# The rows of the residual scaled by their norm on ScalarE in place of VectorE

## The chip, the cores and the metric

One core of a Trainium2 chip runs the whole program. The metric is the device time of one execution in microseconds (us). The time before is the median of three runs.

## The reference

One layer of a backbone for 128 context tokens and 2048 latent tokens, 17 tiles of 128 rows, with 1024 features. What matters here is the second half of the block, and within it the norm:

```python
def rmsnorm(x, w):
    xf = x.astype(jnp.float32)
    y = xf * lax.rsqrt(jnp.mean(xf * xf, axis=-1, keepdims=True) + EPS)
    return (y * w).astype(x.dtype)

x = x + ga1 * o                                        # o: the mixer's output projection
h = rmsnorm(x, norm_ffn_l) * (1.0 + sc2) + sh2
x = x + ga2 * (jnp.square(jax.nn.relu(h @ w_ff1_l)) @ w_ff2_l)
```

The mixer ahead of it runs a gated delta rule over chunks in both directions (the scans) beside a chunked gating MLP. After the block comes one more norm.

## The kernel before

**Stages.** The program first projects all tokens, then scans the sequence forwards and backwards, and last runs the MLP. The backward scan goes through the tiles from 16 down. With each tile it finishes the mixer's output (gate, transposes, output projection, residual add), and for the tiles 16 to 9 it also makes the operands of the MLP. For the tiles 8 to 0 the operands are made in the MLP stage, between the products for the tiles above.

**The MLP's operands.** `h2_steps` makes them for one tile, in steps: the squares of the residual rows and their sum (L836, ScalarE), the sum and rsqrt (L844 and L177 on VectorE, L178 on POOL, which leaves `r`, one number for a row), the scaling of two half rows of 512 by `r` (`scale2`, L849), four transposes on TensorE for each half (L856), and a scale and bias for each feature on the way out of PSUM (L859). The transposed tiles are then combined in pairs (L880), split into a high and a low part (`opH` by a cast on ScalarE, L874; `opL` by a subtraction on VectorE, L875) and stored to DRAM (L877), from where the MLP loads them as `hop`.

**Splits.** Matrix products run three times, high by high, high by low and low by high (L220, L221, L222). So every operand has a cast on ScalarE and a subtraction on VectorE.

**What surrounds the scaling in the scan stage.** On VectorE: `L1437` and `L1438` multiply the output projection by its gate and add it to the residual rows `x`; `L1395` finishes the factors `rr` for the norm of the scan's output, and `L1400` scales that output, `o`, by them (four heads, four instructions); `L1056` and `L1178` belong to the scan (its values, and the masks of the triangular inverse); `L1028` prepares the next chunk. On TensorE: `L1415` transposes `o` and `ob` (the output of the gating MLP); `L1189`, `L1195` and `L1175` are steps of the inverse, `L1062` and `L994` of the scan; `L1246` ends an inverse that `L1239` on VectorE feeds. On ScalarE: `L1419` takes the transposed `o` and `ob` out of PSUM as the high part of the next product (VectorE's `L1420` makes the low part), `L1198` casts the inverse's `Y` and `X` for TensorE, `L1065` copies the scan's `vn`, and `L1021`, `L1022` and `L1067` prepare decay factors.

**What sets the order.** The steps are written in the order of a table of times for each scan step, with some orders between engines set by hand; then a scheduler orders the instructions of all engines by a model of their times. So a step that changes its engine can move other instructions. Each engine runs its instructions in that order, and waits in place for what an instruction needs. All loads and stores are issued on SP's queue.

Of the kernel before, what the change touches and what calls it, by code (L numbers as in the profile page):

```python
# [13 lines left out]
AF = mybir.ActivationFunctionType  # L14
# [48 lines left out]
def hybrid_step(  # L63
# [7 lines left out]
    V, A, G, T = nc.vector, nc.scalar, nc.gpsimd, nc.tensor  # L71
# [9 lines left out]
    def cond(t):  # L81
        return 0 if t == 0 else 1

    def f32(ap):
        return ap.bitcast(F32)
# [88 lines left out]
    def rsqrt_cols(out, ss, n, scale, eps):  # L174
        t = smp.tile([P, 72], F32, tag="rsq", name="rsq", bufs=2)
        np_ = ss.shape[0]
        V.tensor_scalar(out=t[:np_, :n], in0=ss, scalar1=scale, scalar2=eps, op0=ALU.mult, op1=ALU.add)  # L177
        G.tensor_tensor(out=out, in0=t[:np_, :n], in1=nhalf[:np_, :n], op=ALU.pow)  # L178
# [102 lines left out]
    with ExitStack() as ph:  # L281
# [108 lines left out]
        for t in BLOCKS[0]:  # L390
            x = p1.tile([P, D], F32, tag="x", name="x", bufs=3)
# [368 lines left out]
        for bi in range(len(BLOCKS)):  # L760
# [8 lines left out]
            for n, (gi, h) in enumerate(order):  # L769
                u = us[n] if bi == 0 and n < 3 else feature_tile(blk, bi, gi, h)  # L770
# [48 lines left out]
    def h2_steps(t, psum, tmp, wide=w512, part=None, half=None, src=None, own=None):  # L819


        u = {}
        cd = cond(t)
        wide, part, half = wide, part or wide, half or w512

        def rows():
            u["x"] = [wide("x"), wide("x")]
            for n in range(2):
                load(out=u["x"][n], in_=x2_d[t * P : (t + 1) * P, n * 512 : (n + 1) * 512])

        def squares():
            if src:
                u["x"] = src()
            u["ss"] = smp.tile([P, 2], F32, tag="ss2", name="ss2")
            for n in range(2):
                A.activation(tmp(), u["x"][n], AF.Square, accum_out=u["ss"][:, n : n + 1])  # L836
            if t % 2:
                u["y"] = [part("y"), part("y")]
                for h, y in enumerate(u["y"]):
                    load(out=y.rearrange("p (k d) -> p k d", k=4), in_=h2_d[t + 1][:, h * 4 : h * 4 + 4, :])  # L840

        def norm2():
            u["r"] = smp.tile([P, 1], F32, tag="r", name="r")
            V.tensor_tensor(out=u["ss"][:, 0:1], in0=u["ss"][:, 0:1], in1=u["ss"][:, 1:2], op=ALU.add)  # L844
            rsqrt_cols(u["r"], u["ss"][:, 0:1], 1, 1.0 / D, EPS)

        def scale2():
            for n in range(2):
                V.tensor_scalar_mul(u["x"][n], u["x"][n], u["r"])  # L849

        def trans2(half):
            def f():
                ps = psum()
                ev = wide("ev")
                for i in range(4):
                    T.transpose(ps[:, i * P : (i + 1) * P], u["x"][half][:, i * P : (i + 1) * P], ident)  # L856
                for i in range(4):
                    k = half * 4 + i
                    A.activation(ev[:, i * P : (i + 1) * P], ps[:, i * P : (i + 1) * P], AF.Identity,  # L859
                                 scale=a2[:, cd, k : k + 1], bias=b2[:, cd, k : k + 1])  # L860
                if own:
                    own(ev, half)
                elif t in h2_d:
                    store(out=h2_d[t][:, half * 4 : half * 4 + 4, :], in_=ev.rearrange("p (k d) -> p k d", k=4))
                else:
                    u[half] = ev
            return f

        def put(o, src):

            c = (t - 1) % 8 // 2 * P
            dst = hop_d[t <= 8, o][:, :, :, c : c + P]
            h, lo = half("opH", F32R), half("opL", F32R)
            A.copy(h, src)  # L874
            V.tensor_tensor(out=lo, in0=src, in1=f32(h), op=ALU.subtract)  # L875
            for i, piece in enumerate((h, lo)):
                store(out=dst[:, :, i, :], in_=f32(piece).rearrange("p (k d) -> p k d", k=4))  # L877

        def sub(a, b, out=None):
            V.tensor_tensor(out=a if out is None else out, in0=a, in1=b, op=ALU.subtract)  # L880

        def plain():
            put(1, u[0])
            put(2, u[1])
            u["d"] = part("d")
            sub(u["y"][1], u["y"][0], u["d"])

        def third():
            put(3, u["y"][1])
            put(7, u["d"])  # L890
            sub(u["y"][0], u[0])

        def fifth():
            put(5, u["y"][0])
            sub(u["y"][1], u["y"][0])

        def sixth():
            put(6, u["y"][1])
            sub(u[1], u["y"][1])

        def fourth():
            put(4, u[1])

        ops = [plain, third, fifth, sixth, fourth] if t % 2 else []
        return ([] if src else [rows]) + [squares, norm2, scale2, trans2(0), trans2(1)] + ops

    def sraw():
# [19 lines left out]
    with ExitStack() as ph:  # L927
# [551 lines left out]
        for i, u in enumerate(units):  # L1479
# [9 lines left out]
            if c == 0:  # L1489
# [3 lines left out]
                n = len(steps)  # L1493
# [118 lines left out]
    class Unit:  # L1612
# [6 lines left out]
        def load(self, i, kh):  # L1619
            for q in range(2):  # L1620
                self.raw[i, kh, q] = r = w512("raw")
                r0, c0 = kh * 512 + q * 256, self.jp * 512 + i * 256
                load(out=r.rearrange("p (a c) -> p a c", a=2),
                     in_=w_ff1[0, r0 : r0 + 256, c0 : c0 + 256].rearrange("(a p) c -> p a c", p=P))
# [354 lines left out]
    for p, (o, n, m) in enumerate(seq):  # L1979
        u = units[n]  # L1980
# [126 lines left out]
```

## Time and profile before

| | |
|---|---|
| median of 3 runs | 2574.07 us (2570.79 to 2575.09) |
| the profiled execution | 2574.06 us |
| its span, from the first to the last instruction | 2572.3 us |
| TensorE (PE) busy | 2536.5 us |
| VectorE (DVE) busy | 1782.1 us |
| ScalarE (ACT) busy | 1192.8 us |
| GpSimd (POOL) busy | 315.1 us |
| granted TensorE clock | 0.999 |

In the rows below, a name such as L849 is a line of the kernel, and `out<-in` are tiles. A row of the timeline starts with the time in the span and the length in us; a bracket at its end is the time for which its engine had been idle, and what released it. A row of the waits gives who waited for whom, the sum in us, the number of times, and the longest. A row of a group of instructions gives the busy time in us and the mean of one in ns, then the idle time ahead of them and its releasers. An engine's idle time matters only where another engine waits for it in the end.

### The profile page before, as it was taken

To read this page: it belongs to the slowest core of one execution; us is meant where nothing else is said; L and a number is where in the kernel's file an instruction comes from. 1 tells how busy PE (TensorE), PEld (TensorE's weight loads), DVE (VectorE), ACT (ScalarE), POOL (GpSimd) and SP (SyncE) were. 2 spreads that over 40 slices of the span, in tenths; PEclk is the share of its full clock that TensorE was granted. 3 is DMA by queue.
4 is the path that set the end of the run, shared out by engine and by line. 5 is a ranking of instruction groups with operands and counts; after the bars stand their busy time and mean duration, and the time that the engine had idled before them with its cause. 6 is when DMAs were issued, how large, how long until landed. Compare 5 with 4: busy or idle time off the path is not lost.

```text
span 2572.3 us, 43717 instructions
## 1 busy us (share of the span) xinstructions
PE 2536.5 (99%) x15296; PEld 2132.5 (83%) x15296; DVE 1782.1 (69%) x3525; ACT 1192.8 (46%) x2758; POOL 315.1 (12%) x512
## 2 busy tenths in 40 slices
PE   8999999999999999999999999999999999999998
PEld 4999999788888788778888888888888888888887
DVE  5777746667667788885587886677674445684874
ACT  4755545554545566763355553333243333243441
POOL 3112112222222233331000000000000000000000
PEclk9999999999999999999999999999999999999999
DMA  8966637755556758896778788445599778686773
GB/s 285 299 225 205 191 126 219 246 161 171 171 169 179 228 185 270 279 304 209 274 219 249 221 289 279 140 147 152 180 299 323 267 258 296 241 259 211 232 253 105
DMA packets 533859, 579.77 MB, mean 225 GB/s; under 512 B 35500, under 2 KB 366684, under 8 KB 530054
## 3 DMA queue, kind: packets, MB, share of 16 engines
q1 hardware_dynamic: 533638, 576.98, 69.3%
q8 instruction: 120, 1.97, 0.3%
q14 instruction: 101, 0.83, 0.1%
HBM read 397.62 MB, written 179.22 MB: 224 GB/s over the span
## 4 chain that ended last, share of the span: by engine, by line
PE 55%; DVE 1%; issue 1%; DMA 0%; ACT 0%; POOL 0%; DVEq 0%; POOLq 0%; ACTq 0%
PE f L220 17%; PE f L221 17%; PE f L222 17%; PE pj L220 1%; PE pj L222 1%; PE pj L221 1%; PE f L856 0%; PE pd L994 0%; PE pd L1098 0%; PE pd L1099 0%; DMA hop_d<-opL 0%; PE pm L1415 0%; PE pd L1062 0%; PE f L270 0%; PE f L1738 0%
## 5 line engine op out<-in xcount | busy, mean ns | idle before, releaser
L220 PE MATMUL f<-hop,zH 128*128 128x512 f32 x960 | 373.2, 389 | 0.0
L222 PE MATMUL f<-hop,zL 128*128 128x512 f32 x960 | 373.1, 389 | 0.0
L221 PE MATMUL f<-hop,zH 128*128 128x512 f32 x960 | 373.1, 389 | 0.0
L220 PE MATMUL f<-hop,wH 128*128 128x512 f32 x896 | 351.4, 393 | 0.0
L221 PE MATMUL f<-hop,wH 128*128 128x512 f32 x896 | 348.9, 390 | 0.0
L222 PE MATMUL f<-hop,wL 128*128 128x512 f32 x896 | 344.3, 390 | 0.0
L1601 ACT CAST zH<-zraw 128x512 fp32r<-128x512 f32 x240 | 146.3, 620 | 286.1 <-DVE zraw L1595 87.4
L1595 DVE TENSOR_TENSOR zL<-zraw,zH 128x512 fp32r<-128x512 f32 x240 | 162.2, 687 | 77.6 <-ACT zH L1601 66.1
L221 PEld LDWEIGHTS f<-hop,zH 128*128 128x128 f32 x960 | 180.2, 188 | 37.4
L222 PEld LDWEIGHTS f<-hop,zL 128*128 128x128 f32 x960 | 180.2, 188 | 37.4
L220 PEld LDWEIGHTS f<-hop,zH 128*128 128x128 f32 x960 | 180.2, 188 | 37.3
L222 PEld LDWEIGHTS f<-hop,wL 128*128 128x128 f32 x896 | 168.2, 188 | 35.7
L220 PEld LDWEIGHTS f<-hop,wH 128*128 128x128 f32 x896 | 168.5, 188 | 33.9 <-issue 0.9
L221 PEld LDWEIGHTS f<-hop,wH 128*128 128x128 f32 x896 | 168.5, 188 | 32.2
L222 PE MATMUL pj<-kH,wL 128*128 128x386 f32 (+2 forms) x568 | 190.5, 335 | 0.0
L220 PE MATMUL pj<-kH,wH 128*128 128x386 f32 (+2 forms) x568 | 189.2, 336 | 0.5 <-DVE kH L487 0.3
L221 PE MATMUL pj<-kL,wH 128*128 128x386 f32 (+2 forms) x568 | 189.3, 333 | 0.0
L178 POOL TENSOR_TENSOR r<-rsq,nhalf 128x1 f32<-128x1 f32 (+1 forms) x38 | 23.0, 605 | 1351.8 <-DVE rsq L177 1351.8
L1748 ACT CAST wH<-s 128x512 fp32r<-128x512 f32 x96 | 58.9, 620 | 172.5 <-DVE s L1595 156.9
L537 DVE SCALAR_TENSOR_TENSOR cv<-pj,vec,cv 128x384 f32<-128x384 f32 (+2 forms) x164 | 87.1, 539 | 56.9 <-ACT cv L534 55.5
L220 PEld LDWEIGHTS pj<-kH,wH 128*128 128x128 f32 x568 | 107.1, 189 | 5.1 <-issue 4.7
L221 PEld LDWEIGHTS pj<-kL,wH 128*128 128x128 f32 x568 | 107.4, 189 | 0.5
(409 smaller groups left out, 5726.5 us busy)
## 6 DMA issues: line engine op xcount, KB each, us to landing
zraw<-z_d SPq DMA_DIRECT2D x212, 256.0 KB
raw<-in_w_ff_dram SPq DMA_DIRECT2D x128, 256.0 KB
hop<-hop_d SPq DMA_DIRECT2D x28, 1024.0 KB
z_d<-c SPq DMA_DIRECT2D x96, 256.0 KB
zraw<-s_d SPq DMA_DIRECT2D x96, 256.0 KB
raw<-in_w_mod_dram SPq DMA_DIRECT2D x80, 256.0 KB
r<-in_w_ff_dram SPq DMA_DIRECT2D x80, 256.0 KB
s_d<-s SPq DMA_DIRECT2D x64, 256.0 KB
```

What stands on the lines that cost most here:

```text
L178: G.tensor_tensor(out=out, in0=t[:np_, :n], in1=nhalf[:np_, :n], op=ALU.pow)
L220: T.matmul(ps, lh, rh, start=first and i == 0, stop=False, skip_group_check=more)
L221: T.matmul(ps, lh, rl, start=False, stop=False, skip_group_check=more)
L222: T.matmul(ps, ll, rh, start=False, stop=last and i == n - 1, skip_group_check=more)
L537: V.scalar_tensor_tensor(out=cv[:, o : o + m], in0=ps[:, s + sh : s + sh + m], scalar=convw[:, w, j : j + 1], in1=cv[:, o : o + m], op0=AL ...
L1595: V.tensor_tensor(out=out, in0=a, in1=b, op=op)
L1601: A.copy(h, src)
L1748: A.copy(h, s2)
```

## The change

The scaling of the two half rows is a `tensor_scalar` of VectorE before; it is an activation of ScalarE after, the function Copy with the column `r` as its scale, in place as before. It stands in `h2_steps`, so it applies to all 17 tiles: 34 instructions.

```diff
         def scale2():
             for n in range(2):
-                V.tensor_scalar_mul(u["x"][n], u["x"][n], u["r"])
+                A.activation(u["x"][n], u["x"][n], AF.Copy, scale=u["r"])
```

The order of the instructions is the same up to the first scaling. After it, it differs at the following kinds of places. Of the eight tiles in the scan stage, take the fourth and the fifth; the sixth and eighth, and the third and seventh, are much like them.

The fourth tile (place A), VectorE, around the end of the output projection. `tmp` and `x` are the projection with its gate and the residual rows of the next tile, `rr` and `o` the factors and the scan's output:

```order
 L1437 TENSOR_TENSOR tmp<-pj,row 128x512
 L1395 SCALAR_TENSOR_TENSOR rr<-rr,rq 128x4
-L849 TENSOR_SCALAR x<-x,r 128x512 x2
 L1438 TENSOR_TENSOR x<-x,tmp 128x512
 L1400 SCALAR_TENSOR_TENSOR o<-o,rr,ga 128x128 x4
```

The two scalings are gone from between, and nothing else moves.

The same place on ScalarE. `Y` belongs to the inverse, `vn` to the scan, `fraw` takes the squares of the next tile's rows, `oH` the high part of the transposed `ob` (first) and `o` (second):

```order
 L1152 CAST Y<-pd 128x512
 L1065 COPY vn<-pd 128x512
+L849 ACTIVATE x<-x,r 128x512 x2
+L836 ACTIVATE fraw,ss_14234<-x 128x512
 L1419 ACTIVATE oH<-pj 128x512
-L836 ACTIVATE fraw,ss_14234<-x 128x512
 L1419 ACTIVATE oH<-pj,vec 128x512
```

The pair comes behind the copy of `vn`, and the squares of the next tile now stand ahead of the first `oH`.

The fifth tile (place B), ScalarE. `gr` are decay factors, `ev` a transposed half of the tile before, `opH` its high part:

```order
 L1198 CAST Y<-pd 128x64x8
 L1198 CAST X<-pd 128x64x8
-L874 CAST opH<-ev 128x512
-L1021 ACTIVATE gr<-gr,gcol 128x128 x4
+L849 ACTIVATE x<-x,r 128x512
+L874 CAST opH<-ev 128x512
+L1021 ACTIVATE gr<-gr,gcol 128x128 x4
+L849 ACTIVATE x<-x,r 128x512
 L874 CAST opH<-ev 128x512
 L1022 ACTIVATE gr<-gr 128x512
```

One scaling stands ahead of each of the two casts `opH`.

The same place on VectorE. `P` takes the masked product of the inverse, `d` is a difference of two transposed halves:

```order
-L849 TENSOR_SCALAR x<-x,r 128x512
 L880 TENSOR_TENSOR d<-y 128x512
 L1395 SCALAR_TENSOR_TENSOR rr<-rr,rq 128x4
-L849 TENSOR_SCALAR x<-x,r 128x512
 L1056 SCALAR_TENSOR_TENSOR vt<-pd,neg_196,vt 128x128 x4
 L875 TENSOR_TENSOR opL<-ev,opH 128x512
 L1178 COPY_PREDICATED P_5735<-om_189,pd 128x32x16
+L1400 SCALAR_TENSOR_TENSOR o<-o,rr,ga 128x128 x4
+L1437 TENSOR_TENSOR tmp<-pm,row 128x512
 L875 TENSOR_TENSOR opL<-ev,opH 128x512
-L1437 TENSOR_TENSOR tmp<-pm,row 128x512
-L1400 SCALAR_TENSOR_TENSOR o<-o,rr,ga 128x128 x4
```

The scalings leave, and the four L1400 move ahead of L1437 and of the second `opL`.

On TensorE, the four transposes of `o` stand four matmuls sooner at place B and at the two places like it, and three matmuls sooner for the second tile; in the MLP stage some products trade places with their neighbours. On POOL, two instructions of one chunk trade places. On SP's queue, loads and stores that stand next to each other trade places: a load of `gr` with a store of `x2`, stores of `opH` with stores of `opL`. Nothing else is added or taken away on any engine.

## The prediction

> **What bounds the kernel now.** I read the busy totals of the page first, then the waits of TensorE in the part of the span where the changed line runs, then busy time by stretch, and last the timeline around each wait.
>
> ```profile
> PE 2536.5 (99%) x15296; PEld 2132.5 (83%) x15296; DVE 1782.1 (69%) x3525; ACT 1192.8 (46%) x2758; POOL 315.1 (12%) x512
> ```
>
> TensorE is busy for 2536.5 of 2572.3 us. Nothing can be gained but from the 35.8 us in which it idles, and the change leaves the count and the shapes of its instructions alone. The line itself, and the stretches it runs in:
>
> ```profile
> L849 DVE TENSOR_SCALAR x<-x,r x34: 470/480/1257, 949.2 to 1493.7; 128x512 f32<-128x512 f32 x34
> ```
>
> ```profile
> 1000.00:1050.00 50.00, 48.22 (x449) 39.81 (x446) 43.80 (x96) 37.78 (x99) 22.05 (x19) 1.00 0.88 275
> 1050.00:1100.00 50.00, 48.19 (x433) 40.17 (x432) 43.62 (x95) 37.30 (x101) 21.28 (x16) 1.00 0.92 286
> 1100.00:1150.00 50.00, 47.32 (x418) 38.76 (x417) 42.68 (x94) 31.63 (x87) 16.46 (x14) 1.00 0.98 316
> 1250.00:1300.00 50.00, 50.00 (x226) 41.43 (x225) 31.58 (x52) 20.49 (x42) 0.55 (x1) 1.00 0.94 324
> ```
>
> The columns after the length are PE, PEld, DVE, ACT and POOL busy, then granted clock, DMA share and GB/s. Line 849 runs for 17 tiles, twice each: tiles 16 to 9 in the scan stage (949 to 1109 us), where TensorE idles about 2 us in 50, VectorE is busy 85 to 88% and ScalarE 63 to 76%; and tiles 8 to 0 in the MLP stage (1284 us on), where TensorE is busy all the time. So the change can pay or cost only in the first half of its places. The waits of TensorE between 940 and 1210 us, all of them:
>
> ```profile
> PE pj L1415 <- DVE o L1400: 3.8, 3, 1.3
> PE pd L1246 <- DVE R L1239: 1.3, 2, 1.1
> PE pd L1189 <- DVE P L1178: 1.1, 4, 0.4
> ```
>
> 6.2 us in nine waits, each of them for VectorE. This is the most that the change can give; everything after stands in line behind TensorE, so a gap that closes here moves the end by as much.
>
> **The change part by part: the three waits of 1.2 to 1.3 us (place A).** The tile scaled at 1018 us, with the two like it:
>
> ```profile
> 1017.82 0.55 POOL L178 TENSOR_TENSOR r<-rsq,nhalf 128x1 f32<-128x1 f32 x1
> 1018.40 2.02 DVE L849 TENSOR_SCALAR x<-x,r 128x512 f32<-128x512 f32 x2 [0.36 <-POOL r L178]
> 1018.93 1.20 POOL L1043 TENSOR_TENSOR vt<-vt,hbeta 128x512 f32<-128x512 f32 x1
> 1020.34 0.68 DVE L1438 TENSOR_TENSOR x<-x,tmp 128x512 f32<-128x512 f32 x1
> 1020.49 0.40 PE L222 MATMUL pm<-wH,oL 128*128 128x512 f32 x1
> 1020.94 1.13 DVE L1400 SCALAR_TENSOR_TENSOR o<-o,rr,ga 128x128 f32<-128x128 f32 x4
> 1022.12 0.66 PE L1415 MATMUL pj<-ident,o 128*128 128x128 f32 x4 [1.24 <-DVE o L1400]
> ...
> 1066.59 0.66 PE L1415 MATMUL pj<-ident,o 128*128 128x128 f32 x4 [1.26 <-DVE o L1400]
> ...
> 1111.05 0.66 PE L1415 MATMUL pj<-ident,o 128*128 128x128 f32 x4 [1.26 <-DVE o L1400]
> ```
>
> Here the pair of scalings takes 2.02 us of VectorE, not twice 0.48, because the second one runs beside POOL's L1043 and takes 1.26 (the 1257 of the line's row). Behind it on VectorE stand only L1438 and the four L1400, and the transposes of TensorE wait for these. Without the pair, L1438 starts 2.02 + 0.36 us sooner if nothing else holds it; I count 2.02. That is 0.78 more than the gap of 1.24, so the transposes follow L222 with no wait. Gain: 3.8 us for the three.
>
> The SBUF page of the Trainium skill (section "Who interferes with whom") says that a VectorE instruction in a two-port mode and a GpSimd instruction exclude each other for their whole length, and that ScalarE waits for neither. The row of 470 against 1257 agrees for VectorE; no run here yet shows the ScalarE half. By the rule the whole 2.02 leaves VectorE and comes to ScalarE without the stretch.
>
> What the pair costs on ScalarE is not in the trace. The nearest rows:
>
> ```profile
> L1748 ACT CAST wH<-raw 128x512 fp32r<-128x512 f32 x112 | 68.0, 622 | 5.2 <-DMA raw<-in_w_ff_dram 5.2
> L1419 ACT ACTIVATE oH<-pm,vec 128x512 fp32r<-128x512 f32 x12 | 8.2, 687 | 6.3 <-PE pm L1415 6.1
> L1419 ACT ACTIVATE oH<-pm 128x512 fp32r<-128x512 f32 x12 | 7.2, 597 | 16.9 <-PE pm L1415 16.9
> L308 ACT ACT_TABLE_LOAD x1 | 1.3, 1283 | 0.8 <-PEq L2093 0.8
> ```
>
> The same width from SBUF costs 622 ns; a scale column adds 687 - 597 = 90. So about 0.71 us for one; bounds 0.62 (no extra for the column) and 1.26 (if it were stretched as VectorE's is). I take 0.71, since the 687 row is the same function with a scale column. It is Copy with a scale, which L1419 runs already, and the program loads its table once, so no load is added. The ScalarE page (section "What ACT_TABLE_LOAD costs") gives 186 ns, plus 93 for the pointer, plus 0.833 for each of 512 elements; that is an estimate of 706, in agreement with 710.
>
> At place A, ScalarE has room for 1.42 us:
>
> ```profile
> 1017.38 0.59 ACT L1065 COPY vn<-pd 128x512 f32<-128x512 f32 x1 [0.36 <-PE pd L1062]
> 1019.21 0.60 ACT L1419 ACTIVATE oH<-pj 128x512 fp32r<-128x512 f32 x1 [1.24 <-PE pj L1415]
> 1021.05 0.63 ACT L836 ACTIVATE fraw<-x 128x512 f32<-128x512 f32 x1 [1.24 <-DVE x L1438]
> 1022.82 0.69 ACT L1419 ACTIVATE oH<-pj,vec 128x512 fp32r<-128x512 f32 x1 [1.04 <-PE pj L1415]
> ```
>
> Now the pair stands behind L1065, and L836 ahead of L1419. r lands at 1018.37; the pair would run to 1019.8, L836 (x then ready since about 1018.8) with its read of the accumulator to 1020.6, the first L1419 to 1021.2, where it ended at 1019.8. Its reader on VectorE, L1420, comes behind L1400 and L1178, at about 1020.6, so it waits 0.6 there, still ending before its old time of 1022.6 and with nothing of TensorE behind it. The second L1419 starts when its transposes are done, about 1021.6, not 1022.82. The three idle stretches of ScalarE (1.24, 1.24, 1.04) cover the pair. If that cover were gone, the price is 1.42 a place.
>
> **The waits for L1178 (place B).** The tile scaled at 1035 us; those at 991 and 1080 are alike:
>
> ```profile
> 1035.08 0.49 DVE L849 TENSOR_SCALAR x<-x,r 128x512 f32<-128x512 f32 x1 [1.46 <-POOL r L178]
> 1035.29 0.64 ACT L874 CAST opH<-ev 128x512 fp32r<-128x512 f32 x1
> 1036.15 0.48 DVE L849 TENSOR_SCALAR x<-x,r 128x512 f32<-128x512 f32 x1
> 1036.55 1.12 DVE L1056 SCALAR_TENSOR_TENSOR vt<-pd,neg,vt 128x128 f32<-128x128 f32 x4
> 1038.03 1.27 ACT L1067 ACTIVATE kt<-kt,eglg 128x128 f32<-128x128 f32 x4
> 1038.18 0.68 DVE L1178 CAST_PREDICATED P<-om,pd 128x512 f16<-128x512 uint16 x1
> 1038.92 0.39 PE L1189 MATMUL pd<-P,X 128*128 128x64 f16 x8 [0.31 <-DVE P L1178]
> 1039.35 0.59 ACT L1198 CAST Y<-pd 128x512 f16<-128x512 f32 x1
> 1042.18 0.40 PE L1175 MATMUL pd<-Y,AH 128*128 128x64 f16 x8
> 1042.38 0.60 ACT L1419 ACTIVATE oH<-pm 128x512 fp32r<-128x512 f32 x1 [1.24 <-PE pm L1415]
> ```
>
> VectorE here loses the wait for r (1.46) and twice 0.48 ahead of L1178. L1056 then starts when its product is there, about 1 us sooner, and the 0.31 closes. On ScalarE one scaling now stands ahead of each of the two opH casts, so all from L1021 to the cast Y at 1039.35 is later by up to 1.42. Y would end at about 1041.4, and its reader, L1175, runs at 1042.18; the wait of 1.24 ahead of L1419 takes up the rest. What is late next: the hop stores of opH, 0.7 to 1.4 us later in SP's queue, with the load of vt (L1011) behind them:
>
> ```profile
> SPq L1011 <- PE pd L1062: 5.0, 6, 2.7
> ```
>
> That load waits 0.8 us on the mean for a product to free its buffer in any case, so I cost the lateness at nothing; its upper bound is 0.6 a place. All four waits for L1178 go (the fourth stands at 1027 us, behind place A, on a VectorE that is behind there as well): 1.1 us.
>
> The other moves. The transposes L1415 of o stand 3 or 4 matmuls sooner at four places, 0.22 us each (50.00 us for 226), so at most 0.9. Their L1400 is sooner by more than that at the three places B (VectorE runs it ahead of two other 0.68 us instructions besides losing the pair), so nothing is lost. Scalings issue no DMA; the stores and loads that trade places in SP's queue are neighbours, and I cost them at nothing. In the MLP stage 18 scalings add 18 x 0.71 = 12.8 us to a ScalarE that is busy 20.5 of 50 us, with weights made 5 steps ahead and 8 PSUM banks: zero while the row of 50.00 holds.
>
> **What stays.** The wait of 1.3 us at 1144 us comes from elsewhere:
>
> ```profile
> 1143.28 0.69 DVE L875 TENSOR_TENSOR opL<-y,opH 128x512 fp32r<-128x512 f32 x1 [1.40 <-DMA hop_d<-opL]
> ```
>
> VectorE waits there for a store to leave its buffer, in the stretch with a DMA share of 0.98. All work ahead comes up to 4.9 us sooner, the DMA work is the same, and a queue that is so full need not keep up: the wait may grow by 0 to 4.9. I take 0.7, half of the 1.40, since the stretches ahead (0.88, 0.92) still have 10 us of DMA slack in 100.
>
> **Sum.** -3.8 - 1.1 + 0.7 = -4.2 us against the profiled execution's 2574.06 us (span 2572.3 and 1.76 around it), which is the median of the three runs, 2574.07, to 0.01. That gives 2569.9 us, 0.16% less.
>
> **The rivals.**
> 1. The DMA takes the gain back. For it: the share of 0.98, the 1.40 above. Against: no TensorE wait but the last two of the nine goes back to a DMA. Then the 1.3 grows by most of 4.9: about 2573.5 us.
> 2. All nine waits go, since opL's buffer is also free sooner when its store is issued sooner: -6.2, so 2567.9 us. Against: that wait is for a landing, not for VectorE's work.
> 3. Slower: ScalarE becomes what TensorE's chain waits for. If the in-order ScalarE stands waiting for r ahead of the casts X and Y (L1198), each of the eight scan tiles pays a pair, 8 x 1.42 = 11.4 us, less the 4.9 gained: +6.5, so 2580.6. It decides where a pair costs more than the 1.0 to 1.2 us of room between Y's end and L1175, that is where r comes later than the casts ahead of it. Against: at place B r had landed when L849 started at 1035.08, before ScalarE was free for opH at 1035.29.
> 4. Nothing closes, because L1400 waits for something beside VectorE's backlog: 2574 us. Against: what L1438 and L1400 read (tmp, rr) is written by instructions that stand ahead of the pair on VectorE, and the releaser of the three waits is L1400 itself.
>
> **How the numbers follow.** Forecast 0.55, rival 1 0.19, rival 2 0.13, rival 3 0.06, rival 4 0.07. About 0.2% (5.1 us) is what a measurement of this kernel can tell from no change: the three runs lie within 4.3. The forecast is 1 us above the line at 2568.9, so of its chance I give 0.16 to faster and 0.39 to same; rival 2 gives 0.10 and 0.03; 1 and 4 are same; 3 is slower. Faster 0.26, same 0.68, slower 0.06. The range runs from 2567.2 (rival 2 with 0.7 for the spread of a median) to 2574.6 (rival 4 with 0.6), and leaves out rival 3 and the tails.
>
> **What the changed profile would show.** L849 on ACT, 34 times, 0.6 to 0.75 us each, VectorE about 19 us less busy and ScalarE about 23 more; no wait of L1415 for L1400 at 1022, 1066 and 1110 us; no wait of L1189 for L1178; the wait at L1246 still there, 1 to 3 us; TensorE still at 50.00 of 50 in the MLP stage. A TensorE wait for ACT Y or X (L1198) would show rival 3; a wait at L1246 of 4 us or more, rival 1. The prediction is wrong if ScalarE takes 1.2 us for one scaling, or if a new wait for r heads its queue.

## The result, and the profile after

The kernel after took 2568.22 us (median of 9 runs, 2564.42 to 2570.62) beside 2574.07 us for the kernel before (9 runs, 2570.79 to 2575.55): 0.9979 of the time, with a 95% interval of 0.997 to 0.9988. Measured once more among the experiments it came to 2569.09 us beside 2572.82, 0.9988 (0.9979 to 0.9997). So it is faster, by 0.12 to 0.21%. The forecast was 2569.9 us.

The busy totals on the page of the profiled execution (2568.22 us, span 2566.1), and the changed line:

```profile
PE 2535.4 (99%) x15296; PEld 2131.9 (83%) x15296; DVE 1771.7 (69%) x3491; ACT 1212.2 (47%) x2792; POOL 315.1 (12%) x512
```

```profile
L849 ACT ACTIVATE x<-x,r x34: 707/723/765, 949.2 to 1488.7; 128x512 f32<-128x512 f32 x34
```

TensorE's busy time is the same to 1.1 us; the span is 6.2 us shorter, because gaps of TensorE closed. A scaling takes 0.72 us on ScalarE, as forecast (0.71). The stretches of before, now:

```profile
1000.00:1050.00 50.00, 49.81 (x454) 41.27 (x453) 43.85 (x94) 40.58 (x104) 22.55 (x18) 1.00 0.94 288
1050.00:1100.00 50.00, 49.82 (x444) 41.22 (x444) 43.76 (x99) 41.09 (x112) 17.86 (x15) 1.00 0.95 300
1100.00:1150.00 50.00, 48.60 (x439) 40.40 (x438) 43.97 (x92) 31.92 (x80) 17.28 (x16) 1.00 0.99 317
```

In the first two stretches TensorE idled 1.8 us each before, and idles 0.2 now. VectorE is no less busy than it was (43.85 against 43.80): the scalings have left these stretches, L1400 takes longer (below), and later work has moved up. The waits of TensorE between 940 and 1210 us after (in us: sum, times, longest), all of them:

```profile
PE pd L1246 <- DVE R L1239: 1.2, 2, 1.0
PE pd L1189 <- DVE P L1178: 0.3, 2, 0.2
```

Before, there were 6.2 us in nine waits; 1.5 us in four are left. The three waits of L1415 for L1400 are gone.

To compare executions I cut the span in three: up to the last matmul of L1320 (mostly projections; the changed line comes later, but L1043 of e8 to e11 begins in it), from there to the last one of L1062 (the part of the scan stage in which the changed line runs), and the rest. The ends are the last starts in the rows of those two lines. Before, then after:

```profile
L1320 PE MATMUL pj<-vg,wsT x32: 270/275/356, 495.6 to 906.4; 128*128 128x128 f32 x32
L1062 PE MATMUL pd<-vt,T x272: 270/275/356, 512.0 to 1206.6; 128*128 128x128 f32 x136
```

```profile
L1320 PE MATMUL pj<-vg,wsT x32: 270/275/356, 494.6 to 905.3; 128*128 128x128 f32 x32
L1062 PE MATMUL pd<-vt,T x272: 270/275/356, 511.0 to 1199.8; 128*128 128x128 f32 x136
```

| kernel | to the last L1320 | scan part | rest | span |
|---|---|---|---|---|
| before | 906.4 | 300.2 | 1365.7 | 2572.3 |
| after | 905.3 | 294.5 | 1366.3 | 2566.1 |
| after, second time (e12) | 906.9 | 294.5 | 1366.5 | 2567.9 |
| e1: only the scan tiles | 907.6 | 294.1 | 1365.9 | 2567.6 |
| e2: only the MLP tiles | 904.2 | 300.2 | 1366.8 | 2571.2 |
| e3: only scan tiles with odd numbers | 904.7 | 296.5 | 1365.7 | 2566.9 |
| e4: only scan tiles with even numbers | 903.5 | 299.0 | 1366.0 | 2568.5 |
| e5: only the second half row | 903.3 | 297.6 | 1365.7 | 2566.6 |
| e6: ScalarE's part done twice | 904.0 | 296.5 | 1369.5 | 2570.0 |
| e8: e1, and half of L1043 on ScalarE | 905.8 | 294.8 | 1365.8 | 2566.4 |
| e9: before, and half of L1043 on ScalarE | 904.5 | 300.3 | 1365.7 | 2570.5 |
| e10: before, and all of L1043 on ScalarE | 903.8 | 300.3 | 1366.0 | 2570.1 |
| e11: after, and all of L1043 on ScalarE | 905.0 | 295.8 | 1366.4 | 2567.2 |

The first part, in which no scaling stands, lies between 903.3 and 907.6 us, nearly as far apart as single executions of before as a whole (2570.79 to 2575.55). So I compare the parts behind it. The scan part is 294.5 us in both profiles of after, which is in part chance, as e12 shows below. So the change takes 5.7 us from the scan part and gives back 0.6 to 0.8 in the rest: 5.0 us, 0.19%, which both intervals hold.

### The profile page after: what moved, and what is told of

The parts are those of the page before. It is cut to its first block, busy times and chain, and to the rows that moved or that the text cites. A ratio compares the mean times of both kernels' runs of the same rounds, so it can differ in the third digit from the quotient of the medians.

```text
span 2566.1 us, 43746 instructions
## 1 busy us (share of the span) xinstructions
PE 2535.4 (99%) x15296; PEld 2131.9 (83%) x15296; DVE 1771.7 (69%) x3491; ACT 1212.2 (47%) x2792; POOL 315.1 (12%) x512
## 4 chain that ended last, share of the span: by engine, by line
PE 74%; DVE 2%; DMA 1%; ACT 1%; issue 1%; POOL 0%; SPq 0%; DVEq 0%; POOLq 0%; ACTq 0%
PE f L220 17%; PE f L221 17%; PE f L222 17%; PE pj L220 3%; PE pj L222 3%; PE pj L221 3%; PE pd L994 2%; PE pm L220 1%; PE pm L222 1%; PE pm L221 1%; PE pd L1098 1%; PE pd L1099 1%; PE pd L1062 1%; PE pd L1189 1%; PE pd L1195 1%
## 5 line engine op out<-in xcount | busy, mean ns | idle before, releaser
L222 PE MATMUL f<-hop,zL 128*128 128x512 f32 x960 | 373.1, 389 | 0.0
L222 PE MATMUL f<-hop,wL 128*128 128x512 f32 x896 | 344.2, 390 | 0.0
L222 PEld LDWEIGHTS f<-hop,zL 128*128 128x128 f32 x960 | 180.2, 188 | 37.4
L222 PEld LDWEIGHTS f<-hop,wL 128*128 128x128 f32 x896 | 168.2, 188 | 35.7
L222 PE MATMUL pj<-kH,wL 128*128 128x386 f32 (+2 forms) x568 | 190.5, 335 | 0.0
```

Source lines behind the costliest of these rows:

```text
L222: T.matmul(ps, ll, rh, start=False, stop=last and i == n - 1, skip_group_check=more)
```

## The experiments

The theory: VectorE ahead of the transposes L1415 is the bound of the scan part, and the pair of scalings leaves it. The rivals: the gain comes from elsewhere (the order of other instructions, the DMA), or from the stretch of L849 beside POOL alone; and the MLP stage may pay or gain. Each run was timed in five rounds (11 executions, 6 of e8). "Before" is the time of the kernel before on the same chip in that round of runs: 2571.63 us for e1 to e4, 2573.4 for e5 to e9, 2572.82 for e10 to e12.

**Which tiles (e1, e2).** The line of the kernel after, restricted to the tiles of the scan stage (e1) or of the MLP stage (e2):

```diff
-A.activation(u["x"][n], u["x"][n], AF.Copy, scale=u["r"])
+A.activation(u["x"][n], u["x"][n], AF.Copy, scale=u["r"]) if t > 8 else V.tensor_scalar_mul(u["x"][n], u["x"][n], u["r"])
```

> ScalarE scales the rows of the eight scan-stage tiles only; the nine of the MLP stage stay on VectorE. Theory 1 (the gain is TensorE's waits for VectorE in the scan stage): the waits of L1415 for L1400 are gone, TensorE reaches its last scan product about 5.8 us sooner measured from 949 us, and the time is 5.8 to 6.4 us below before, 0 to 0.6 better than the full change. Rival (part of the gain was made in the MLP stage, by a freer VectorE there): less than 5 us.

> ScalarE scales the rows of the nine MLP-stage tiles only. Theory 1: no TensorE wait goes, so no change, between 0 and 0.6 us slower, since the full change showed TensorE losing about 0.6 us between 1280 and 1610 us. Rival (the MLP stage gains): 1 us or more faster.

e1: 2567.3 us, 0.998 (0.9971 to 0.9989). e2 (the same with `t <= 8`): 2573.91 us, 1.0008 (0.9999 to 1.0017). The whole gain is in the scan tiles; the scan part of e2 is before's 300.2. The MLP tiles don't come free: the rest is 1366.8 in e2, against 1365.7 before. The place is one matmul, here in after, then the same matmul in e2 (rows of the timeline):

```profile
1434.43 1.04 POOL L178 TENSOR_TENSOR r<-rsq,nhalf 128x1 f32<-128x1 f32 x1 [27.53 <-ACT opH L874]
1435.50 1.34 ACT L849 ACTIVATE x<-x,r 128x512 f32<-128x512 f32 x2 [0.64 <-POOL r L178]
1436.75 0.60 ACT L874 CAST opH<-y 128x512 fp32r<-128x512 f32 x1
1437.26 0.62 ACT L874 CAST opH<-d 128x512 fp32r<-128x512 f32 x1
1437.69 0.39 PE L222 MATMUL f<-hop,wL 128*128 128x512 f32 x1
1437.78 0.57 ACT L1677 COPY x<-f 128x512 f32<-128x512 f32 x1
1438.40 0.50 PE L220 MATMUL f<-hop,wH 128*128 128x512 f32 x1 [0.33 <-ACT x L1677]
```

```profile
1443.23 0.50 PE L220 MATMUL f<-hop,wH 128*128 128x512 f32 x1 [0.56 <-ACT x L1677]
```

ScalarE stands 0.64 us waiting for `r`, then runs the pair for 1.34 and two casts, and the copy L1677 stands behind these. That copy takes product 1 out of its bank of PSUM, and product 2 is added onto that same bank (`self.product(2, m, 1)`), so it can't start before. Other banks are no help to it.

**Which place (e3, e4).** Scan tiles with odd numbers are places A, those with even numbers are places B:

```diff
-A.activation(u["x"][n], u["x"][n], AF.Copy, scale=u["r"])
+A.activation(u["x"][n], u["x"][n], AF.Copy, scale=u["r"]) if t > 8 and t % 2 else V.tensor_scalar_mul(u["x"][n], u["x"][n], u["r"])
```

> ScalarE scales only the scan-stage tiles with odd numbers. These are the places A, where the pair ran beside POOL on VectorE and stood right ahead of L1400. Theory 1: the three waits of 1.24 to 1.26 us at L1415 go, with the one of 0.16 behind them; 3.6 to 4.6 us faster, and the three waits of 0.3 us at L1189 stay. Rival (place A and place B only pay together, since VectorE's lateness runs from one into the next): under 2.5 us faster.

> ScalarE scales only the scan-stage tiles with even numbers, the places B. Theory 1: the three waits of 0.3 us at L1189 go, the three waits at L1415 stay at about 1.25; 1 to 2 us faster. Rival (lateness runs on): the waits at L1415 shrink too, and it is 3 us or more faster.

e3: 2569.74 us, 0.9991 (0.9982 to 0.9999). e4 (`t % 2 == 0`): 2570.17 us, 0.9991 (0.9982 to 1.0). The two can't be told apart by their times; the waits of TensorE between 940 and 1210 us tell them apart, e3 first:

```profile
PE pd L1189 <- DVE P L1178: 1.4, 6, 0.3
PE pd L1246 <- DVE R L1239: 0.8, 2, 0.5
```

```profile
PE pj L1415 <- DVE o L1400: 3.7, 3, 1.2
PE pd L1246 <- DVE R L1239: 1.5, 2, 1.3
PE pd L1189 <- DVE P L1178: 0.4, 2, 0.3
```

Places A close the waits of L1415 and leave those for L1178; places B do the opposite. The scan part is 3.7 us shorter with A and 1.2 with B; 4.9 of the 6.1 of e1. The other 1.2 lies outside of these places. From issue to issue (counted below, with the prediction), the stalls at places A are 3.6 us shorter in e3 and those at and behind places B 2.0 in e4, together after's 5.7. The rest are waits ahead of the first scaling and at L1246, which differ from execution to execution.

**The stretch beside POOL (e5).** Only the second half row goes to ScalarE, which is the one that ran beside POOL's L1043:

```diff
-A.activation(u["x"][n], u["x"][n], AF.Copy, scale=u["r"])
+A.activation(u["x"][n], u["x"][n], AF.Copy, scale=u["r"]) if n else V.tensor_scalar_mul(u["x"][n], u["x"][n], u["r"])
```

> The second half of the rows is scaled on ScalarE, the first stays on VectorE, for all 17 tiles. At place A VectorE keeps one scaling of 0.48 and loses the one that POOL's L1043 stretched to 1.26. Theory (what counts is how far L1400 is late behind what stands ahead of it, the collision with POOL included): the three waits at L1415 fall from 1.25 to 0.5 or less, and the stage from 905 to 1200 us shortens by 2.5 to 4 us. Rival (each scaling counts its own 0.48, and the collision is beside the point): the waits fall by 0.48 only, to about 0.8, and the stage shortens by about 1.5.

2571.48 us, 0.9991 (0.9982 to 1.0). The scan part is 2.6 us shorter, as the theory had it, but the waits of L1415 sum to 2.7 us, 0.9 each, so there the rival's number came out. The timeline at place A says why:

```profile
1015.19 0.84 DVE L849 TENSOR_SCALAR x<-x,r 128x512 f32<-128x512 f32 x1 [0.36 <-POOL r L178]
1015.72 1.20 POOL L1043 TENSOR_TENSOR vt<-vt,hbeta 128x512 f32<-128x512 f32 x1
1015.95 1.52 DVE L1438 TENSOR_TENSOR x<-x,tmp 128x512 f32<-128x512 f32 x1
1018.58 0.66 PE L1415 MATMUL pj<-ident,o 128*128 128x128 f32 x4 [0.91 <-DVE o L1400]
```

The stretch did not leave with the second scaling. L1438, which took 0.68 us in before, stands there now and takes 1.52 beside the same L1043. So the stretch goes with the instruction that VectorE runs beside L1043, and not with L849. In the kernel after it has moved one instruction further, to the L1400. There the first of the four takes 0.72 us beside POOL's L1039, the second 1.12 beside L1043, and the other two 0.34:

```profile
1016.23 0.69 DVE L1438 TENSOR_TENSOR x<-x,tmp 128x512 f32<-128x512 f32 x1
1016.61 0.39 PE L222 MATMUL pm<-wH,oL 128*128 128x512 f32 x1
1016.67 1.34 ACT L849 ACTIVATE x<-x,r 128x512 f32<-128x512 f32 x2 [0.43 <-POOL r L178]
1016.83 2.29 DVE L1400 SCALAR_TENSOR_TENSOR o<-o,rr,ga 128x128 f32<-128x128 f32 x4
1016.84 0.60 PE L1415 MATMUL pj<-ident,ob 128*128 128x128 f32 x4
1017.38 1.07 POOL L1043 TENSOR_TENSOR vt<-vt,hbeta 128x512 f32<-128x512 f32 x1
1018.75 0.40 PE L222 MATMUL pm<-wH,oL 128*128 128x512 f32 x1
1019.18 0.66 PE L1415 MATMUL pj<-ident,o 128*128 128x128 f32 x4
```

Four L1400 take 2.29 us there, 1.13 in before: 1.16 of the 2.02 that left VectorE is back at each of the three places. The pair on ScalarE runs beside L1043 as well and isn't stretched (1.34, the same as in the MLP stage above, where no L1043 runs).

This run also tells VectorE's time from the order of the instructions. At places B those of VectorE and TensorE stand as in before, but for the one scaling that is gone, and L1189 starts 0.30 us behind the matmul ahead of it, where it started 0.71 behind in before (1038.21, 1038.92) and 0.24 in after:

```profile
1035.27 0.40 PE L222 MATMUL pm<-wH,oL 128*128 128x512 f32 x1
1035.51 0.41 PE L1189 MATMUL pd<-P,X 128*128 128x64 f16 x8
```

So less work on VectorE is enough to close the wait at place B, without the other moves there. At place A nothing else moves on VectorE in any case.

**The stretch taken away (e9, e8, e10, e11).** L1043 itself goes to ScalarE, as four activations with a scale column, in the backward units (`d == 1`); in e9 and e8 with the further condition `t > 8`:

```diff
-G.tensor_tensor(out=u["vt"], in0=u["vt"], op=ALU.mult,
+[A.activation(u["vt"][:, h, :], u["vt"][:, h, :], AF.Copy, scale=col(hbeta, h)) for h in range(H)] if d == 1 else G.tensor_tensor(out=u["vt"], in0=u["vt"], op=ALU.mult,
```

> The kernel before, all scalings on VectorE, but POOL's L1043 of the backward scan units of tiles 16 to 9 is replaced by four activations of ScalarE (Copy with a scale column, 128x128 each), so that POOL has nothing to collide with at place A. Theory (the collision is over half of the cost at place A): no scaling takes 1.26 us, the pair at place A takes 0.9, the three waits at L1415 fall from 1.25 to 0.1 to 0.4, the waits at L1189 stay, and the stage from 905 to 1200 us shortens by about 3 us. Rival (the gain needs VectorE free of the pair): the waits at L1415 stay above 0.8.

> Scaling on ScalarE for the scan-stage tiles only, and L1043 of those units on ScalarE too, in place of POOL. In the full change L1400 ran beside L1043 and took 2.29 us in place of 1.13, so the collision only moved. Theory (a stall of 0.2 us, shorter than the rows can show, is left at each place A): L1400 takes 1.13 again, the stage from 905 to 1200 us is 0.5 to 1 us shorter than with scaling alone, and the time is 0 to 1 us below it. Rival (ScalarE, then 86% busy or more in the stage, becomes late): new TensorE waits for ScalarE, and 1 us or more slower than with scaling alone.

e9: 2572.24 us, 0.9996 (0.9987 to 1.0005). e8: 2566.47 us, 0.9972 (0.996 to 0.9985). In neither did the scan part get shorter (300.3 and 294.8), against what I expected. For what closed, ScalarE made new waits: L1212 waits 0.8 us for its Y in e9, L1222 0.6 for its R in e8. The condition is another reason: the units run some tiles ahead of the scaling, so `t > 8` moved L1043 only up to 1023.6 us, which takes it from one place A of three. At that one the wait of 1.24 us fell, at the next it didn't (e9):

```profile
1021.47 0.65 PE L1415 MATMUL pj<-ident,o 128*128 128x128 f32 x4 [0.46 <-DVE o L1400]
...
1065.63 0.66 PE L1415 MATMUL pj<-ident,o 128*128 128x128 f32 x4 [1.25 <-DVE o L1400]
```

So I ran it for all backward units, on before and on after:

> The kernel before, with L1043 of every backward unit on ScalarE (four activations with a scale column), where the run before moved it only up to 1023.6 us of the span and so took it from one of the three places A. At that place the wait of L1415 fell there from 1.24 to 0.46 us, at the other two it stayed at 1.25. Theory (the wait is the length that L1043 on POOL adds to the pair of scalings): all three waits of L1415 for L1400 fall to 0.4 to 0.5 each, 1.2 to 1.5 in all, where they were 3.8; no L849 is longer than 0.85 us; the scan stage is 2 to 2.5 us shorter than before's 300.2, unless ScalarE makes a new wait. Rival (the waits come from the length of the whole chain on VectorE, and the first place was chance): the other two stay at 1.2 us each, sum 3.0, stage 300.

> The kernel after, with L1043 of every backward unit on ScalarE. Theory (the change moved the collision with POOL from L849 to L1400, and that still hides up to 0.2 us of stall at each place A): the four L1400 beside POOL take 1.1 to 1.6 us where they took 2.29 (no single one over 0.7 us), VectorE is about 3 us less busy in the scan stage, and the stage is 0.6 us shorter than after's 294.5 at the most; the time is the same as after's within 1 us. Rival (ScalarE, now 1.26 us busier in each unit, is late for the inverse): waits of TensorE for ACT Y, X or R of 0.5 us or more, and a stage that is 1 to 5 us longer than after's.

e10: 2574.08 us, 1.0006 (0.9997 to 1.0015). Its waits of TensorE between 940 and 1210 us:

```profile
PE pd L1212 <- ACT Y L1198: 2.4, 3, 0.8
PE pj L1415 <- DVE o L1400: 1.4, 3, 0.5
PE pd L1222 <- ACT R L1215: 1.1, 4, 0.3
PE pd L1189 <- DVE P L1178: 0.7, 3, 0.3
```

The waits of L1415 are 1.4 us where they were 3.8, and the longest L849 is 845 ns: the stretch beside L1043 was 0.78 us of each wait of 1.24, and the pair's own length and a shorter stretch beside POOL's L1039 make the 0.46 that is left. But nothing is gained: the four activations make ScalarE late with the casts Y and R of the inverse, and the new waits (2.4 and 1.1, and one of 0.6 us for Y at 917 us, ahead of the listed stretch) take it all. The scan part is 300.3 us.

e11: 2568.03 us, 0.998 (0.9971 to 0.9989). All L1400 between 940 and 1210 us, in after and in e11 (busy us, then mean ns of one), and e11's waits:

```profile
L1400 DVE SCALAR_TENSOR_TENSOR o<-o,rr,ga 128x128 f32<-128x128 f32 x52 | 20.3, 450 | 0.0
```

```profile
L1400 DVE SCALAR_TENSOR_TENSOR o<-o,rr,ga 128x128 f32<-128x128 f32 x52 | 16.3, 374 | 0.0
```

```profile
PE pd L1222 <- ACT R L1215: 2.0, 4, 0.6
PE pd L1246 <- DVE R L1239: 0.9, 2, 0.6
```

The stretch beside L1043 is gone from L1400 too, with 4.0 us of VectorE's time; the one beside L1039 is left (0.73 to 0.74 us for one L1400 at each place A). The transposes follow without a stall, and the wait of 0.15 for L1178 behind them is gone as well. But in this run the four L1400 also stand ahead of L1437 and L1438 at places A, so it doesn't show which of the two closed them. ScalarE is late for R instead, and the scan part is 1.3 us longer than after's: the rival's lower end.

**How much ScalarE can take (e6).** Each half is scaled, then copied once more:

```diff
 A.activation(u["x"][n], u["x"][n], AF.Copy, scale=u["r"])
+A.activation(u["x"][n], u["x"][n], AF.Copy, scale=1.0)
```

> As the full change, but each half row is passed through ScalarE once more, with a scale of 1; ScalarE's work for the scaling is doubled, from 0.72 to 1.44 us a half. Theory (ScalarE's room is 1.4 us at place A and about 1 at place B, so a pair fits and two pairs do not): TensorE waits for ScalarE appear (L1198 or L1419 at places A and B, L1677 in the MLP stage), and the time is 2 to 6 us above the full change. Rival (ScalarE has room for twice that): within 1.5 us of the full change.

2571.91 us, 0.9992 (0.9983 to 1.0001): most of the gain is gone. In the scan part (2.0 us longer than after's) L1175 now waits for Y; in the MLP stage the same matmul as above waits longest:

```profile
PE pd L1175 <- ACT Y L1198: 0.7, 3, 0.2
```

```profile
1440.67 0.50 PE L220 MATMUL f<-hop,wH 128*128 128x512 f32 x1 [1.80 <-ACT x L1677]
```

So rival 3 of the prediction is a mechanism that exists; a pair of 1.34 us stays under it in the scan stage, two pairs do not.

**The result once more (e12).** The kernel after, unchanged, beside e10 and e11.

> The kernel after once more, on this chip and beside the same runs of before as the other two. Theory: 0.997 to 0.999 of before; the stage 294.5 us within 0.4, in which the L849 is 0.72 us on ScalarE, and the listed waits of TensorE in it sum to 1.5 us; from the scan stage's end to the end of the span 0.3 to 0.9 us longer than before's 1365.7. Rival (the gain of the first measurement was the spread of the part before 905 us): the stage within 1 us of before's 300.2.

2569.09 us, 0.9988 (0.9979 to 0.9997). The scan part is 294.5 us again and the rest 1366.5. The listed waits are not the expected 1.5 us, however:

```profile
PE pd L1189 <- DVE P L1178: 0.6, 3, 0.3
PE pd L1246 <- DVE R L1239: 0.2, 1, 0.2
```

That is 0.8 us, for a part of the same length. The wait at L1246 is shorter by 0.9 us, counted from issue to issue, and two waits ahead of the first scaling, one of them outside of the listed stretch, are new here and cost the same 0.9:

```profile
936.62 0.66 PE L1415 MATMUL pm<-ident,o 128*128 128x128 f32 x4 [0.29 <-DVE o L1400]
943.61 0.40 PE L1189 MATMUL pd<-P,X 128*128 128x64 f16 x8 [0.28 <-DVE P L1178]
```

So the equal length of 294.5 is a coincidence of these two; what repeats are the places A and B, which run alike in both executions. e1 (2567.3) and e8 (2566.47) are not measurably faster than after. e1 leaves out the 0.6 to 0.8 us of the MLP stage, which is below what the medians can tell.

## Why the prediction was right, and where not

**Places A: the waits closed, by errors that cancel.** All three waits of L1415 closed, and e3 shows that the tiles with odd numbers close them; rival 4, in which nothing closes, is out. The step's spare was not as counted. I had taken all of 2.02 us off VectorE, 0.78 more than the wait; but 1.16 of it comes back as the stretch of L1400. By the prediction's own numbers the wait should then have shrunk by 0.86 only. It did close: L1438 starts sooner by 2.02 + 0.36, for the wait for `r` ahead of the pair left VectorE too, and I had left that 0.36 out. 2.02 + 0.36 - 1.16 = 1.22, which is the wait of 1.24 almost to the last. The trace shows the rest: L1415 issues 0.43 us behind L222 (1018.75, 1019.18), where the normal distance is 0.23 (1016.61, 1016.84). So 0.2 us of stall is left, and no row names it. The step came out by two errors that cancel, which is luck: with the stretch alone it would have left 0.4 us of each wait.

The Trainium skill, page "SBUF — State Buffer", section "Who interferes with whom", has the rule that I had passed over: beside the two-port modes, a VectorE instruction with both inputs in SBUF contends with a GpSimd instruction that reads SBUF. L1438 and L1400 have two such inputs, and the runs agree: 1.52 us for 0.68, and 2.29 for 1.13. That ScalarE waits for neither, as the same section says, is shown here by the 1.34 us of the pair beside L1043.

**Places B: right; the fourth wait stayed.** The three waits of 0.30 to 0.35 us at places B are gone, and e4 ties this to the tiles with even numbers. I had counted on all four for L1178; the one behind place A stays (0.16 us at 1027.65 before, 0.15 at 1024.70 now), and one like it behind another place A makes the 0.3 that are listed. On ScalarE the cast Y ends 0.66 us ahead of L1175 (1038.12, 1038.78), where it ended 2.24 ahead in before and I had 0.8: the pair fits, with little to spare.

**The gain in the scan part: undersized.** The sum had 4.9 us from the waits; the part is 5.7 shorter. The listed waits fell by 4.7. What is missing lies in how a wait is listed: the profile models the end of a matmul about 0.17 us past the issue of the next (0.40 us for one, with 0.23 from issue to issue), so the row of 1.24 at 1022.12 in before stands for 1.63 from L222 to L1415, a stall of 1.40. And a short stall makes no row in the list. So I count the same matmuls from issue to issue. At places A, L1415 follows 1.63 us behind L222 before and 0.43 after; at places B, L1189 0.71 and 0.24; and behind places B, L1222 follows 0.44 us behind its L222 before (1048.64, 1049.08) and 0.24 after (1045.18, 1045.42). That makes 1.2, 0.5 and 0.2 us at each, three places each: 5.7 us, the whole of it. The last 0.6 I hadn't seen, as it is in no list. It is still there in e5 (1044.70, 1045.13), where the order at places B is that of before, so it may come from the transposes that moved up in after; no run has tried that alone.

**The wait at L1246: the step failed.** I had it grow by 0.7, as a queue that can't keep up. The same instruction of VectorE in after, and the matmul behind it:

```profile
1136.46 0.69 DVE L875 TENSOR_TENSOR opL<-y,opH 128x512 fp32r<-128x512 f32 x1 [1.35 <-DMA hop_d<-opL]
1137.81 0.38 PE L1246 MATMUL pd<-R,X 128*128 128x128 f16 x4 [1.00 <-DVE R L1239]
```

Counted from the last L1320 the instruction starts 5.7 us sooner (1143.28 - 906.4 = 236.9 before, 231.2 now), and its wait is 1.35, as 1.40 before. The store came sooner by just what the rest did, at a DMA share of 0.98 before and 0.99 now. In e12 the same wait was 0.47. So rival 1 is out, and rival 2, in which it closes, didn't come either. The listed waits at L1246 are 1.2 and 0.2 us in the two executions of after, and between none and 1.5 over all the runs. What a further buffer would do was not tried.

**The MLP stage: the step failed, by a small size.** I had costed it at zero, "with weights made 5 steps ahead and 8 PSUM banks". It costs 0.6 and 0.8 us in the two executions of after and 1.1 in e2. Most of it is at the one product that is added onto a bank still to be copied: it follows the matmul ahead after 0.71, 0.83 and 0.95 us, where 0.23 is usual. The rest isn't located, and that part of the span differs by up to 0.3 us among the runs without scalings of ScalarE in it. The stage's mean of 20.5 busy us in 50 said nothing of the one place where ScalarE's order matters.

**ScalarE: the price was right, and a sign of being wrong came.** 0.72 us for one; 1.34 for a pair, as two that follow each other overlap. The busy totals moved by less than I said, VectorE by 10.4 for 19 and ScalarE by 19.4 for 23; 3.9 of VectorE's is the stretch of L1400, and I haven't traced the rest. I had called a new wait for `r` at the head of ScalarE's queue a sign that the prediction is wrong. It came: 0.43 us at place A and 0.64 at the product above. At place A ScalarE's idle time takes it up (0.78 us are left ahead of the second L1419, 1.04 in before); in the MLP stage it is part of what makes L1677 late.

The sum by what was measured: -5.7 + 0.6 or 0.8, so -5.1 to -4.9, where the forecast was -4.2. The terms of +0.7 for L1246, which didn't come, and of zero for the MLP stage, which cost as much, cancel, and that is luck; the gain from the waits was 0.8 larger.

## What to carry to other kernels

Where an in-order engine is the bound, look at what stands behind the instruction that leaves: a stretch beside another engine falls to the next one in line, and counts against the gain. The engine that takes the work over pays at the few places where something in its queue is waited for, so look for these (a bank that is copied out and then added to, a cast in a chain), not for its mean load. Compare the distance from issue to issue as well as listed waits, and the places that change rather than the whole: the part ahead of the first scaling varied by 4 us, and even in the changed stage waits at other places moved by 0.9 us from one execution to the next.

## What was not expected of the hardware

- In e6 the stall of TensorE at 1440.67 (2.19 us from the matmul ahead, normally 0.23) was followed by slow matmuls, 0.63 us each from 1442.54 on, and a lower granted clock (the column after the five busy times):

```profile
1442.20:1444.20 2.00, 2.00 (x6) 1.57 (x5) 2.00 (x4) 1.47 (x3) 0.00 (x0) 0.50 1.01 286
1444.20:1446.00 1.80, 1.80 (x9) 1.35 (x7) 1.80 (x4) 0.00 (x0) 0.00 (x0) 0.60 1.00 314
```

  2.0 us at 0.50 and 1.8 at 0.60 lose 1.7 us, and the stall is 1.5 longer than in after (0.71 from the matmul ahead there): together the 3.2 us by which e6's rest is longer. Between 1209 and 1560 us the timelines of before, after and e2 have no row of a single matmul of that width at this length. That the stall caused the lower clock is likely by their order, but it was seen once and isn't shown.
- VectorE's `L1400`, 0.34 us alone, took up to 1.14 beside POOL's `L1043` and 0.72 to 0.74 beside its `L1039`; ScalarE's `L849` was between 0.71 and 0.77 us in all 34 places.
